# A two-layer hybrid attention block on one core: ones products in float32r pairs, a stacked gate product, scale sums on GpSimd, head openings issued one head ahead, and a reordered attention tail

## Chip, core and metric

The kernel runs on one core of one Trainium2 chip, in one launch. The metric is device microseconds (us) of an execution. TensorE is called PE here, VectorE DVE, ScalarE ACT, GpSimd POOL; SP is SyncE, which issues nearly all DMAs.

## What is computed

The reference is a block of two layers on 512 tokens of width 1024. Each layer adds a mixer of three branches to the residual stream and then a SwiGLU feed-forward. What matters here are the two linear attention branches, HGRN2 (4 heads of 128 gates and 128 values) and GLA (4 heads of 64 keys and 128 values), which share one recurrence, and the sparse branch NSA that follows them:

```
def chunked_gated_linear_attention(q, k, v, log_g):      # per head
    b = cumsum(log_g)                                    # inside a chunk
    o = (q * exp(b)) @ state + (scores with decay exp(b_t - b_s), causal) @ v
    state = exp(b_last) * state + (k * exp(b_last - b)).T @ v
y_hg  = head_rmsnorm(o_hg,  hg_norm_g)  * silu(hog)
y_gla = head_rmsnorm(o_gla, gla_norm_g) * silu(gog)
log_a = log_sigmoid(glr @ gla_w2 + gla_b) / 16           # glr: 16 columns
y_nsa = compressed + selected + window attention of 8 heads, gated
x = x + (g0*(y_hg@w_hg) + g1*(y_gla@w_gla) + g2*(y_nsa@w_nsa)) @ w_out
x = x + swiglu(rmsnorm(x))
```

## The kernel before

Activations lie transposed (features on partitions, 512 tokens along the free axis). A **dense product** is one 128x512 tile of a projection. Operands are kept as a float32r pair (a rounded part and the remainder), so each 128x128 block of weights costs three matmuls of 512 columns (`mm3`, L262 to L273). All these matmuls are chained in program order through `dense_last`. Weights come over SP as 512 KB pieces (`weights`, L167); ACT rounds a piece (`whi`, L277), DVE subtracts (`wlo`, L278), and both have two buffers.

`layer` (L519) writes the program down head by head, and a list scheduler puts each engine's instructions in order by program position and readiness; each engine then runs its list strictly in that order. Dense products are the filler: while DVE and ACT prepare a head, PE works on projections of later parts. `done` (L589, L623) is called when a head's output product is issued, and decides which projections are written there; `fill` (L568) takes steps from a list of gate and branch projections.

A head of linear attention goes so. `fit` (L361) squares the queries on ACT, sums over partitions with a product of a 128x128 matrix of ones (L368) and turns the sum into a scale. `attend` (L386) multiplies Q and K, sums the product over partitions with ones again (L399: that is the diagonal of the scores), and then works through seven levels of block sizes 1 to 64 (`gated`, L402): ACT rounds halves of K and Q to float16 (L409), DVE forms the remainders (L411) and multiplies gates into K, Q and F (L413 to L415). Levels are taken in pairs; each pair gives 24 small matmuls per head (L427), whose results DVE copies into the score tile under a mask (L433). Three links between the four chunks follow (L437 to L439), then the products of whole chunks (L445, L448) and the output product (L454). `finish` (L458) squares the output, sums it with ones (L465), and multiplies norm and gate. The buffers of a level (`ahl`) are four, so that two pairs can be ready before PE has used one.

Three of these products are plain float32: the diagonal (L399, whole 128 rows in HGRN2, two halves of 64 rows in GLA), the head norm (L465) and the scale sum (L368). The GLA decay is a float32 product over 16 rows (L616) of the low-rank projection, which `small` (L723) transposes (L751).

In NSA (`nsa`, L775) units of one head and one branch pass through scores (L919), softmax (L933), a transposing DMA of the probabilities on SP (`turn`, L952 to L955) and the products with V (`values`, L967), eight units later. After the last unit of a token block `stop` (L977) scales the block (L980) and transposes it on PE (L983). The residual x is read back over SP for the output projection (L637), as soon as its tile (shared with the NSA queries) is free.

## Time and profile before

| what | value |
|---|---|
| median of 3 runs | 1937.19 us (1936.92, 1937.19, 1939.85) |
| the profiled execution, its own time | 1939.51 us |
| its span, first to last instruction | 1937.7 us, so 1.8 us lie around it |
| mean granted TensorE clock | 0.997 |
| PE busy | 98% of the span, 10656 matmul records |
| DVE, ACT, POOL busy | 61%, 52%, 2% |
| layer 0: HGRN2, GLA, NSA | roughly 55 to 230, 230 to 345, 345 to 530 us |
| layer 1: HGRN2, GLA, NSA | roughly 1012 to 1192, 1192 to 1307, 1307 to 1490 us |

The busy time of PE is the union of records whose ends are modelled: a record of 0.39 us of a 512-column matmul overlaps the next, which starts 0.23 us later. So what a matmul costs is read from one start to the next, not from the length of its record. A matmul that was issued and could not yet run also counts as busy.

### The profile page before, as it was taken

To read this page: it belongs to the slowest core of one execution; us is meant where nothing else is said; L and a number is where in the kernel's file an instruction comes from. 1 tells how busy PE (TensorE), PEld (TensorE's weight loads), DVE (VectorE), ACT (ScalarE), POOL (GpSimd) and SP (SyncE) were. 2 spreads that over 40 slices of the span, in tenths; PEclk is the share of its full clock that TensorE was granted. 3 is DMA by queue.
4 is the path that set the end of the run, shared out by engine and by line. 5 is a ranking of instruction groups with operands and counts; after the bars stand their busy time and mean duration, and the time that the engine had idled before them with its cause. 6 is when DMAs were issued, how large, how long until landed. Compare 5 with 4: busy or idle time off the path is not lost.

```text
span 1937.7 us, 27737 instructions
## 1 busy us (share of the span) xinstructions
PE 1891.1 (98%) x10656; PEld 1361.3 (70%) x10656; DVE 1179.1 (61%) x2392; ACT 1009.0 (52%) x1815; POOL 33.5 (2%) x82
## 2 busy tenths in 40 slices
PE   8999999999999999999999999999999999999998
PEld 6778776777788544468887877767777874444787
DVE  5768767778765644423338687677896665444223
ACT  5556544377744755422245466543786457553222
POOL 0000000000000000000000000000000000000000
PEclk9999999999999999999999999999999999999999
DMA  4222211348832633113332222123487335330232
GB/s 156 77 69 86 78 57 61 109 92 158 186 94 90 209 98 107 44 60 108 109 104 66 80 77 68 64 79 96 99 169 169 98 114 190 99 106 14 76 98 96
DMA packets 142293, 194.23 MB, mean 100 GB/s; under 512 B 91408, under 2 KB 94032, under 8 KB 142160
## 3 DMA queue, kind: packets, MB, share of 16 engines
q1 hardware_dynamic: 141584, 191.80, 35.1%
q8 instruction: 84, 1.38, 0.3%
q10 hardware_dynamic: 576, 0.66, 0.1%
q14 instruction: 49, 0.40, 0.1%
HBM read 167.25 MB, written 4.19 MB: 88 GB/s over the span
## 4 chain that ended last, share of the span: by engine, by line
PE 82%; DVE 11%; ACT 3%; DMA 2%; issue 2%; SPq 0%; DVEq 0%; ACTq 0%
PE mmf L266 8%; PE mmf L264 8%; PE mmf L265 8%; PE mm L264 6%; PE mm L266 6%; PE mm L265 6%; PE mmmgate L264 4%; PE mmmgate L266 4%; PE mmmgate L265 4%; DVE wlo L278 2%; PE s L919 2%; PE o L454 2%; DVE ahl L411 2%; DMA lr<-ahl 2%; DVE at L433 1%
## 5 line engine op out<-in xcount | busy, mean ns | idle before, releaser
L277 ACT ACTIVATE whi<-wraw 128x1024 fp32r<-128x1024 f32 (+3 forms) x242 | 232.5, 961 | 359.0 <-PE mm L265 122.3
L278 DVE TENSOR_TENSOR wlo<-wraw,whi 128x1024 fp32r<-128x1024 f32 (+3 forms) x242 | 266.4, 1101 | 173.8 <-ACT whi L277 167.3
L266 PE MATMUL mmmgate<-xg,wlo 128*128 128x512 f32 x384 | 153.4, 400 | 0.4 <-DVE wlo L278 0.4
L264 PE MATMUL mmmgate<-xg,whi 128*128 128x512 f32 x384 | 153.6, 400 | 0.0
L265 PE MATMUL mmmgate<-xg,whi 128*128 128x512 f32 x384 | 153.1, 399 | 0.0
L210 DVE SCALAR_TENSOR_TENSOR whi<-xg,gsc,whi 128x1024 f16<-128x1024 f32 x38 | 48.8, 1284 | 136.0 <-ACT whi L209 136.0
L409 ACT ACTIVATE ahl<-lq 128x256 f16<-128x256 f32 x168 | 65.2, 425 | 90.3 <-DVE lq L413 57.9
L186 ACT ACTIVATE v<-xg 128x1024 bf16<-128x1024 f32 x76 | 79.9, 1051 | 32.2 <-DMA xg<-w 31.8
L264 PEld LDWEIGHTS mmmgate<-xg,whi 128*128 128x128 f32 x384 | 72.7, 189 | 17.4 <-issue 1.5
L209 ACT ACTIVATE wlo<-xg,gsc 128x1024 f16<-128x1024 f32 x38 | 43.5, 1146 | 77.6 <-PE mmf L266 77.6
L266 PEld LDWEIGHTS mmmgate<-xg,wlo 128*128 128x128 f32 x384 | 72.9, 190 | 14.9 <-DVE wlo L278 1.3
L265 PEld LDWEIGHTS mmmgate<-xg,whi 128*128 128x128 f32 x384 | 72.7, 189 | 13.6 <-issue 0.2
L948 DVE SCALAR_TENSOR_TENSOR ahl<-ld,sums,ahl 128x128 f16<-128x128 f32 (+3 forms) x128 | 66.3, 547 | 15.3 <-ACT ahl L947 14.2
L661 DVE SCALAR_TENSOR_TENSOR ld<-mmf,ginv,ld 128x512 f32<-128x512 f32 x40 | 30.0, 751 | 72.7 <-PE mmf L266 72.6
L947 ACT ACTIVATE ahl<-ld,sums 128x128 f16<-128x128 f32 (+3 forms) x128 | 65.5, 553 | 14.9 <-DMA lr<-ahl 10.6
L130 ACT ACTIVATE ld<-s,nm 128x128 f32<-128x128 f32 (+3 forms) x128 | 65.6, 517 | 13.4 <-DVE nm L938 9.4
L264 PE MATMUL mmn<-whi,xg 128*128 128x512 f32 (+1 forms) x192 | 71.3, 371 | 0.9 <-DVE og L484 0.9
L265 PE MATMUL mmn<-wlo,xg 128*128 128x512 f32 (+1 forms) x192 | 71.5, 373 | 0.0
L266 PE MATMUL mmn<-whi,xg 128*128 128x512 f32 (+1 forms) x192 | 71.5, 373 | 0.0
L411 DVE TENSOR_TENSOR ahl<-lq,ahl 128x256 f16<-128x256 f32 x168 | 67.4, 427 | 2.0 <-ACT ahl L409 1.8
L130 ACT ACTIVATE ld<-mmf,ginv 128x512 f32<-128x512 f32 x40 | 27.4, 685 | 68.9 <-PE mmf L266 68.8
L938 DVE TENSOR_REDUCE nm<-s 128x1 f32<-128x384 f32 (+3 forms) x96 | 56.3, 593 | 6.2 <-PE s L919 5.9
(433 smaller groups left out, 4964.6 us busy)
## 6 DMA issues: line engine op xcount, KB each, us to landing
wraw<-w SPq DMA_DIRECT2D x188, 512.0 KB, 3.6
xg<-w SPq DMA_DIRECT2D x76, 512.0 KB, 3.6
wraw<-w SPq DMA_DIRECT2D x57, 256.0 KB, 2.6
xt<-xT SPq DMA_DIRECT2D x16, 256.0 KB, 4.5
lr<-cw SPq DMA_DIRECT2D x16, 256.0 KB, 5.4
xd<-xt SPq DMA_DIRECT2D x8, 256.0 KB, 2.8
xt<-xd SPq DMA_DIRECT2D x8, 256.0 KB, 4.8
out<-lq SPq DMA_DIRECT2D x8, 256.0 KB, 2.6
```

The lines of the kernel that those rows point to most:

```text
L130: i = self.nc.scalar.activation(out, in_, func, **kw)
L186: self.nc.scalar.activation(self.st("v1", list(x.shape), BF), x, AF.Square, scale=scale, accum_out=ss)
L264: first = mm(out, a[0], b[0], start=start, stop=False)
L265: mm(out, a[0], b[1], start=False, stop=False)
L266: last = mm(out, a[1], b[0], start=False, stop=stop)
L277: nc.scalar.activation(hi, x, AF.Copy)
L278: nc.vector.tensor_tensor(lo, x, hi.bitcast(F32), op=ALU.subtract)
L409: nc.scalar.activation(y, x, AF.Copy)
L411: nc.vector.tensor_tensor(z, x, y, op=ALU.subtract)
L938: nc.vector.tensor_reduce(nm, pv, axis=AX.XY, op=ALU.max, negate=True)
L947: nc.scalar.activation(ahl[:, 0, b], a[:, b], AF.Copy, scale=sums[:, b:b + 1])
L948: nc.vector.scalar_tensor_tensor(ahl[:, 1, b], a[:, b], sums[:, b:b + 1], ahl[:, 0, b], op0=ALU.mult, op1=ALU.subtract)
```

## The change

- The matrix of ones becomes float32r. The HGRN2 diagonal and every head norm round their operand into a pair (one ACT copy and one DVE subtraction) and take two float32r products in place of one float32 product. The GLA diagonals stay float32.
- `fit` sums over partitions on GpSimd (`partition_all_reduce`) and needs no product.
- The small gate product becomes one float32r product over 96 rows: the transposed projection stands three times in rows 0, 32 and 64 (rounded, remainder, rounded), against weights that stand there rounded, rounded and as remainder. The weights are loaded once per layer (three DMAs of 16 KB onto a cleared tile), before it twice.
- The opening of head h+1 (scale, SiLU, gates) is written in head h's `done`, ahead of that head's own projections; the projections of Q and K move one head earlier with it.
- The gate projection of a head and the first part of its sigmoid move ahead of the levels (`outgate`), the links ahead of the last pair's products, and the output leaves PSUM earlier in `finish`.
- The NSA query transposes and the small transposes use the output's PSUM tile (`o`). In NSA a finished block is transposed after the next pair of scores, and the residual's DMAs come after the last transposing DMA.

The diff, cut to what is spoken of:

```diff
-        self.ones = self.cp.tile([P, P], F32, name="ones")
+        self.ones_r = self.cp.tile([P, P], F32R, name="ones")
+        self.ones = self.ones_r.bitcast(F32)
...
 def fit(self, xs, junk=None):
-        ps = self.pt("s", [P, n])
-        nc.tensor.matmul(ps, self.ones, acc, start=True, stop=True)
+        tot = self.st("ft", [P, n])
+        nc.gpsimd.partition_all_reduce(tot, acc, P, bass_isa.ReduceOp.add)
...
 def attend(self, Q, K, F, heads, V, gate, done):
             ps = self.pt("s", [P, T])
-            mm(ps, self.ones[p0:p1], prod[p0:p1], start=True, stop=True)
+            if p1 - p0 == P:
+                hl = [self.st("lr", [P, T], F32R) for _ in range(2)]
+                self.split(*hl, prod)
+                for n in range(2):
+                    mm(ps, self.ones_r, hl[n], start=n == 0, stop=n == 1)
+            else:
+                mm(ps, self.ones[p0:p1], prod[p0:p1], start=True, stop=True)
...
+        xs = [gate(h[2]) for h in heads]
...
             pair = [gated(L) for L in LEVELS[l0:l0 + 2]]
+            if l0 + 2 >= len(LEVELS):
+                nc.vector.tensor_copy(Q[:, 0:P], Q[:, 3 * P:])
+                nc.vector.tensor_scalar(Q[:, 3 * P:], Q[:, 3 * P:], F[:, 2 * P:2 * P + 1], None, op0=ALU.mult)
+                nc.vector.tensor_scalar(K[:, 3 * P:], K[:, 0:P], F[:, P:P + 1], None, op0=ALU.mult)
...
 def finish(self, o, g, inv, kc, xt, tag):
+        x, t = xt
-        sq = self.st("ld", [P, T])
+        sq = self.st("lr", [P, T])
         nc.scalar.activation(sq, o, AF.Square, scale=inv)
+        nc.vector.scalar_tensor_tensor(x, o, gi, x, op0=ALU.mult, op1=ALU.mult)
         ss = self.pt("s", [P, T])
-        nc.tensor.matmul(ss, self.ones, sq, start=True, stop=True)
+        hl = [self.st("lr", [P, T], F32R) for _ in range(2)]
+        self.split(*hl, sq)
+        for n in range(2):
+            nc.tensor.matmul(ss, self.ones_r, hl[n], start=n == 0, stop=n == 1)
...
+        gw2, raw = self.st("gw2", [96, 256], F32R), self.st("ld", [96, 256])
+        nc.gpsimd.memset(raw, 0.0)
+        for r in range(0, 96, 32):
+            nc.sync.dma_start(raw[r:r + 16], io["gw2"][l])
+        nc.scalar.activation(gw2, raw, AF.Copy)
+        nc.vector.tensor_tensor(gw2[64:80], raw[64:80], gw2[64:80].bitcast(F32), op=ALU.subtract)
...
+        hready, gready = [hprep(0)], []
+            def done(o, n, x):
+                if h < 3:
+                    hready.append(hprep(h + 1))
+                if h == 0:
+                    QS = self.nsa_q(Bg, rs)
+                    QK.append(pair(2))
...
-            mm(ps, gw2[:, r * P:(r + 1) * P], glrT, start=True, stop=True)
+            mm(ps, gw2[:, r * P:(r + 1) * P], small[2], start=True, stop=True)
...
         for k in range(KD):
-            nc.sync.dma_start(x[:, k], xd[:, k])
+            self.after(nc.sync.dma_start(x[:, k], xd[:, k]), self.last_turn)
...
             Y = self.st("og", [P, 8, 64])
             nc.scalar.activation(Y, Os[i], AF.Copy, scale=ni)
+            if i == NT - 1:
+                turn_y(i, Y)
...
+            else:
+                waiting.append((i, Y))
...
                 scores(*two)
+                while waiting:
+                    turn_y(*waiting.pop(), two[0]["end"])
```

**Where instructions move: PE, the norm of the last HGRN2 head and the opening of the first GLA pair, layer 0.** Before (`mmmgate` are dense products; `s_2248` is the norm sum, `s_2269` the scale sum, `s_2281` the small gate product):

```order
L266 MATMUL mmmgate_314_2207<-xg_159,wlo_2210 128x512
L465 MATMUL s_2248<-ld_2246,ones 128x512
L368 MATMUL s_2269<-fa_2264,ones 128x2
L616 MATMUL s_2281<-misc_1678,w_332_2279 128x512
L264 MATMUL mmmgate_360_2568<-xg_119,whi_2570 128x512
```

After the change, at the same norm (`s_2387`); `s_2409` and `s_2412` are the GLA diagonals, `mmgog` a gate projection:

```order
L267 MATMUL mmmgate_348_2345<-xg_159,wlo_2348 128x512
L487 MATMUL s_2387<-lr_2388,ones 128x512
L487 MATMUL s_2387<-lr_2389,ones 128x512
L406 MATMUL s_2409<-lr_2406,ones 128x512
L406 MATMUL s_2412<-lr_2406,ones 128x512
L265 MATMUL mmgog_365_2415<-xg_119,whi_2417 128x512
```

The norm is two products, the scale sum is gone from PE, the small gate product stands elsewhere, and the diagonals follow the norm at once, ahead of the gate projection that before came after the levels.

**DVE, between heads 0 and 1 of HGRN2, layer 0.** Before (`og_853`: head 0's gated output, `y_872` its remainder, `lq_263` and `lq_296`: head 1's Q and K, `ahl_905`: its first level):

```order
L475 TENSOR_TENSOR og_853<-og_853,ld_861 128x512
L461 TENSOR_SCALAR gi_1301<-fi_883,sp_68 128x1
L278 TENSOR_TENSOR y_872<-og_853,y_871 128x512
L384 SCALAR_TENSOR_TENSOR lq_263<-lq_263,fs_880,ld_885 128x512
L395 TENSOR_TENSOR ld_899<-lq_263,lq_296 128x512
L278 TENSOR_TENSOR wlo_1087<-wraw_1085,whi_1086 128x1024
L396 TENSOR_TENSOR lq_263<-lq_263,lq_891 128x512
L400 COPY_PREDICATED at_897<-imask,s_902 128x4x128
L411 TENSOR_TENSOR ahl_905<-lq_263,ahl_905 128x256
```

After (`lq_236`, `lq_238`: head 0's Q and K at its links; `lr_967`, `lr_987`: the remainders of the two float32r pairs; `lq_271`, `lq_304`: head 1's Q and K; `ahl_1030`: its first level):

```order
L431 TENSOR_SCALAR lq_236<-lq_236,lq_451 128x128
L432 TENSOR_SCALAR lq_238<-lq_238,lq_451 128x128
L482 SCALAR_TENSOR_TENSOR og_501<-o_670,gi_960,og_501 128x512
L279 TENSOR_TENSOR lr_967<-lr_962,lr_966 128x512
L396 TENSOR_TENSOR lr_982<-lq_271,lq_304 128x512
L479 TENSOR_SCALAR gi_1415<-fi_683,sp_68 128x1
L397 TENSOR_TENSOR lq_271<-lq_271,lq_691 128x512
L279 TENSOR_TENSOR wlo_718<-wraw_716,whi_717 128x1024
L279 TENSOR_TENSOR lr_987<-lr_982,lr_986 128x512
L420 TENSOR_TENSOR ahl_1030<-lq_271,ahl_1030 128x256
```

Head 1's products and first level now follow head 0's links directly; before they came after the rotation of the NSA queries and after head 0's norm was finished.

**SP, the end of NSA in layer 0.** Before (`lr<-ahl` are transposing DMAs, `xt` is the residual, `wraw` are weights):

```order
L955 DMA_TRANSPOSE lr_5468<-ahl_5465 128x8x128
L637 DMA xt_6213<-xT 128x512 x3
L171 DMA wraw_5937<-w 128x1024
L955 DMA_TRANSPOSE lr_5480<-ahl_5477 128x8x128
L955 DMA_TRANSPOSE lr_5524<-ahl_5521 128x8x128
L955 DMA_TRANSPOSE lr_5536<-ahl_5533 128x8x128
L637 DMA xt_6213<-xT 128x512
L955 DMA_TRANSPOSE lr_5580<-ahl_5577 128x8x128
L955 DMA_TRANSPOSE lr_5592<-ahl_5589 128x8x128
L637 DMA xt_6213<-xT 128x512 x3
```

After:

```order
L990 DMA_TRANSPOSE lr_5582<-ahl_5579 128x8x128
L990 DMA_TRANSPOSE lr_5594<-ahl_5591 128x8x128
L990 DMA_TRANSPOSE lr_5638<-ahl_5635 128x8x128
L990 DMA_TRANSPOSE lr_5650<-ahl_5647 128x8x128
L670 DMA xt_6271<-xT 128x512
L172 DMA wraw_5995<-w 128x1024
L670 DMA xt_6271<-xT 128x512 x7
```

All eight loads of the residual now stand behind the last transposing DMA; before, four of them stood ahead of some.

## Rows read from the trace of the kernel before

**Rows 1.** The page's line of busy time: engine, busy us, share of the span, instructions.

```profile
PE 1891.1 (98%) x10656; PEld 1361.3 (70%) x10656; DVE 1179.1 (61%) x2392; ACT 1009.0 (52%) x1815; POOL 33.5 (2%) x82
```

**Rows 2.** The page's chain that ended last, shares of the span by engine.

```profile
PE 82%; DVE 11%; ACT 3%; DMA 2%; issue 2%; SPq 0%; DVEq 0%; ACTq 0%
```

**Rows 3.** Busy time by stretch of layer 0: HGRN2, GLA, NSA to its last wait, and the stretch after that wait. Columns: stretch, its length, busy us of PE, of its weight loads, of DVE, ACT and POOL, granted TensorE clock, DMA share, GB/s.

```profile
55.00:230.00 175.00, 172.15 (x1074) 137.56 (x1073) 132.34 (x309) 98.59 (x193) 2.18 (x6) 1.00 0.24 75
230.00:345.00 115.00, 109.19 (x757) 80.40 (x756) 84.54 (x184) 59.48 (x110) 2.47 (x6) 1.00 0.22 68
400.00:523.00 123.00, 116.22 (x925) 91.83 (x924) 105.92 (x268) 99.50 (x248) 0.00 (x0) 1.00 0.74 145
523.00:530.00 7.00, 6.45 (x46) 4.76 (x46) 3.01 (x4) 3.43 (x5) 0.00 (x0) 0.51 1.07 237
```

**Rows 4.** PE's instructions in order of time around one diagonal product of HGRN2 (L399; one float32 product shows as two records). Columns: start, length, instruction.

```profile
59.99 0.40 PE L264 MATMUL mmn<-whi,xg 128*128 128x512 f32 x1
60.23 1.02 PE L399 MATMUL s<-ld,ones 128*128 128x512 f32 x2
60.69 0.80 PE L265 MATMUL mmn<-wlo,xg 128*128 128x512 f32 x1
61.32 0.39 PE L266 MATMUL mmn<-whi,xg 128*128 128x512 f32 x1
61.55 0.40 PE L264 MATMUL mmn<-whi,xg 128*128 128x512 f32 x1
```

**Rows 5.** The same view where norm, scale sum and small gate product stand together, between HGRN2 and GLA of layer 0.

```profile
229.09 0.40 PE L266 MATMUL mmmgate<-xg,wlo 128*128 128x512 f32 x1
229.32 1.02 PE L465 MATMUL s<-ld,ones 128*128 128x512 f32 x2
230.18 0.28 PE L368 MATMUL s<-fa,ones 128*128 128x2 f32 x2
230.39 1.12 PE L616 MATMUL s<-misc,w 16*128 16x512 f32 x2
231.44 0.50 PE L264 MATMUL mmmgate<-xg,whi 128*128 128x512 f32 x1
231.78 0.40 PE L265 MATMUL mmmgate<-xg,whi 128*128 128x512 f32 x1
```

**Rows 6.** Waits of PE over the whole span: who waited for whom, us in total, times, longest.

```profile
PE s L427 <- DVE ahl L411: 13.1, 20, 1.1
PE o L967 <- DMA lr<-ahl: 6.7, 6, 3.1
PE s L983 <- ACT og L980: 1.7, 2, 1.4
```

**Rows 7.** PE's instructions in order of time at the longest wait for a transposing DMA, at the end of NSA in layer 0. In brackets: idle time before, and what ended it.

```profile
520.02 0.39 PE L265 MATMUL mmmgate<-xg,whi 128*128 128x512 f32 x1
523.55 0.82 PE L967 MATMUL o<-v,lr 128*128 128x64 f16 x12 [3.14 <-DMA lr<-ahl]
...
528.12 0.63 PE L265 MATMUL mmmgate<-xg,whi 128*128 128x512 f32 x1
528.54 0.63 PE L266 MATMUL mmmgate<-xg,wlo 128*128 128x512 f32 x1
528.97 0.63 PE L264 MATMUL mmmgate<-xg,whi 128*128 128x512 f32 x1
```

**Rows 8.** SP's DMA issues in order of time before and in that wait. Columns: start of the first, time to the end of the last issue, what, how many.

```profile
504.43 9.18 SPq L955 DMA_TRANSPOSE lr<-ahl  x6
513.71 1.49 SPq L637 DMA_DIRECT2D xt<-xT  x3
515.36 0.33 SPq L171 DMA_DIRECT2D wraw<-w  x1
516.02 7.62 SPq L955 DMA_TRANSPOSE lr<-ahl  x3
523.69 0.57 SPq L637 DMA_DIRECT2D xt<-xT  x1
```

**Rows 9.** DMA issues of one line: what, queue, how many, median us from issue to landing.

```profile
lr<-ahl SPq DMA_TRANSPOSE x96, 3.4
```

**Rows 10.** Groups of instructions by line and shape over the whole span: count, busy us, mean ns of one, idle time of the engine before them and what ended it.

```profile
L278 DVE TENSOR_TENSOR wlo<-wraw,whi 128x512 fp32r<-128x512 f32 x52 | 35.7, 687 | 12.7 <-ACT whi L277 9.0 <-ACT lr L855 3.7
L277 ACT ACTIVATE whi<-wraw 128x512 fp32r<-128x512 f32 x52 | 32.7, 628 | 43.6 <-PE mmmgate L265 14.8 <-PE mmbr0d L265 12.4 <-PE mmn L266 5.9
L277 ACT ACTIVATE whi<-wraw 128x1024 fp32r<-128x1024 f32 x184 | 194.8, 1058 | 307.9 <-PE mm L265 122.3 <-issue 64.9 <-PE mmmgate L265 37.2
L411 DVE TENSOR_TENSOR ahl<-lq,ahl 128x256 f16<-128x256 f32 x168 | 67.4, 427 | 2.0 <-ACT ahl L409 1.8
L413 DVE TENSOR_TENSOR lq<-lq,lq 128x256 f32<-128x256 f32 x84 | 35.5, 423 | 0.2
L433 DVE COPY_PREDICATED at<-lm,s 128x256 f32<-128x256 uint8 x112 | 54.4, 524 | 0.4 <-PE s L427 0.4
L179 POOL PARTITION_ALL_REDUCE gtot<-gss x42 | 18.8, 447 | 794.0 <-ACT v L186 682.5 <-DVE ld L484 105.6 <-DVE y L278 5.8
```

More of the change, by code (lines that the diff above doesn't have):

```diff
@@ L99, in __init__ @@
         self.table("natural_log_exp_and_others")
-    BUFS = dict(gss=2, gtot=2, ge=2, gsc=2, ginv=3, xt=1, og=2, xg=8, wraw=2, whi=2, wlo=2, y=16, nd=3, lq=8, ld=4, g=1, nm=2, sums=6, f=2, ahl=4, lr=9, w1=2, w2=2, w3=2,
+    BUFS = dict(gss=2, fa=2, fs=2, fi=2, gtot=2, ge=2, gsc=2, ginv=3, xt=1, og=2, xg=8, wraw=2, whi=2, wlo=2, y=16, nd=3, lq=8, ld=4, g=1, nm=2, sums=6, f=2, ahl=4, lr=9, w1=2, w2=2, w3=2,
                 at=2, lv=2, v1=1, v2=1, v3=1, acc=1, rb=1, sc=1,
@@ L384, in silu_to, with attend @@
         nc.vector.scalar_tensor_tensor(out, x, s, t, op0=ALU.mult, op1=ALU.mult)
-    def attend(self, Q, K, F, heads, V, done):
+    def attend(self, Q, K, F, heads, V, gate, done):
         nc, tc = self.nc, self.tc
@@ L436, in attend @@
                         ps[:, n].rearrange("p j (g m) -> p j g m", m=L))
[L437 to L439 removed]
         outs = []
[L441 removed]
+        for (p0, p1, vc), at, x in zip(heads, ATs, xs):
             def kt(n):
@@ L581, in layer, with hprep @@
         Vh = self.evac_v(Bg("hi"), rs)
-        for h in range(4):
+        def hprep(h):
             Q, K = QK[h]
@@ L587, in layer, with gprep @@
             self.hg_gates(l, h, K, F)
[L589 to L608 removed]
+            return Q, K, F, inv
+        def gprep(r):
             Q, K = QKg[r]
@@ L621, in layer, with done @@
             self.act(F, F, AF.Exp, scale=0.0625)
-            def done(o, n):
+            return Q, K, F, inv
+        hready, gready = [hprep(0)], []
+        for h in range(4):
+            Q, K, F, inv = hready.pop(0)
+            def done(o, n, x):
+                nonlocal QS, Vg, small
+                if h < 3:
[3 more added lines that the diff above has]
+                    QK.append(pair(2))
+                if h == 1:
+                    Vg = self.evac_v(Bg("gv"), rs)
+                    QK.append(pair(3))
+                if h == 2:
+                    small = self.small(l, xg, rs)
+                    QKg.append(gpair(0))
+                if h == 3:
+                    gready.append(gprep(0))
+                    QKg.append(gpair(1))
+                if h == 3:
+                    fill(PLAN["hg"])
+                return self.finish(o, sp["hgn"][:, n:n + 1], inv, S14, x, "y")
+            yh += self.attend(Q, K, F, [(0, P, h)], Vh, lambda n: self.outgate(A("hog", n, "og")), done)
+        v12, sg, glrT = small
+        for r in range(2):
+            Q, K, F, inv = gready[r]
+            def done(o, n, x):
+                if n == 0:
+                    gready.append(gprep(1))
                 fill(PLAN["gla"][n])
-                if n == 0:
-                    QKg.append(gpair(1))
-                return self.finish(o, sp["glan"][:, n:n + 1], inv, 1.0, A("gog", n, "og"), "lq")
-            yg += self.attend(Q, K, F, [(0, 64, 2 * r), (64, P, 2 * r + 1)], Vg, done)
+                return self.finish(o, sp["glan"][:, n:n + 1], inv, 1.0, x, "lq")
+            yg += self.attend(Q, K, F, [(0, 64, 2 * r), (64, P, 2 * r + 1)], Vg, lambda n: self.outgate(A("gog", n, "og")), done)
         yn = self.nsa(l, sp, Bg, rs, QS, *v12, sg, fill, steps)
@@ L954, in turn @@
             aT = u["aT"] = self.st("lr", [P, 2, w], F16)
-            nc.sync.dma_start(aT.rearrange("p t (j c) -> p (t j) c", c=P), u["ahl"].rearrange("p t c -> p (t c)"), transpose=True)
+            ins = nc.sync.dma_start(aT.rearrange("p t (j c) -> p (t j) c", c=P), u["ahl"].rearrange("p t c -> p (t c)"), transpose=True)
+            self.last_turn = ins.ins.name
         def values(u):
@@ L980, in stop, with turn_y @@
             nc.scalar.activation(Y, Os[i], AF.Copy, scale=ni)
+            if i == NT - 1:
+                turn_y(i, Y)
+                self.hold = ins.ins.name
+                fill(1)
+            else:
+                waiting.append((i, Y))
+        waiting = []
+        def turn_y(i, Y, end=None):
             pt = self.pt("s", [P, 4, P])
             for c in range(4):
-                tp(pt[:, c], Y[:, 2 * c:2 * c + 2].rearrange("p h d -> p (h d)"), self.ident)
+                ins = tp(pt[:, c], Y[:, 2 * c:2 * c + 2].rearrange("p h d -> p (h d)"), self.ident)
+                if end is not None:
+                    self.after(ins, end)
             c = slice(i * P, (i + 1) * P)
@@ L986, in stop @@
             nc.vector.tensor_tensor(yl[:, :, c], pt, yh[:, :, c].bitcast(F32), op=ALU.subtract)
-            if i == NT - 1:
-                self.hold = ins.ins.name
-                fill(1)
         units = []
```

63 lines of the change are left out of this document (20 added, 43 removed).

## The prediction

> **What bounds the kernel now.** I read the line of busy time first: PE works 98% of the span, DVE 61% [rows 1]. The chain that ended last agrees: 82% of it is PE [rows 2]. A busy record says little about pace here, so the second view is the busy time by stretch. It shows where PE is short of full: 2.9 us in HGRN2 of layer 0, 5.8 us in GLA, 6.8 us in NSA, while DVE has 43, 30 and 17 us to spare in the same stretches [rows 3]. So PE sets the time, and a change pays in two ways: by taking work off PE, or by ending a wait of PE. Work added to DVE or ACT is paid only where PE waits for it.
>
> The third view, PE in order of time, gives prices. A dense matmul of 512 columns starts 0.23 us after the one before (61.32 to 61.55). Around a float32 ones product, 59.99 to 61.55 is 1.56 us and holds three dense matmuls, 0.69 us; the product takes 0.87 us, nearly four dense matmuls [rows 4]. The cluster at the head of GLA starts the scale sum at 230.18, the gate product at 230.39 and the next dense matmul at 231.44: 0.21 us and 1.05 us [rows 5].
>
> The fourth view is PE's waits: 13.1 us for the remainders of levels (20 times), 6.7 us for transposing DMAs, 1.7 us for the scaled NSA block [rows 6]. The longest wait is worth a look in order of time. From 520.02 the next matmul should start at 520.25 and starts at 523.55, 3.3 us late; then dense matmuls stand 0.42 us apart, not 0.23 [rows 7]. The granted clock of 523 to 530 is 0.51, the 1.2 GHz level, after PE had stood idle; in the stretches before it was 1.00 [rows 3].
>
> **The parts, priced.** Both layers are counted, 8 HGRN2 heads and 8 GLA heads in all.
>
> *Diagonal and norm.* A pair of float32r products has the shape of two dense matmuls, 0.46 us. Against 0.87 us that saves 0.41 us, for 8 diagonals 3.3 us and for 16 norms 6.6 us. They cost 24 rounds on ACT of 0.63 us and 24 subtractions on DVE of 0.69 us [rows 10], 15.1 and 16.5 us. I cost these at nothing: 8 of them per layer fall in HGRN2's heads, 5.5 us of DVE out of 43 spare, and PE has dense products in between. If that cover is gone they stand in the chain, 1.32 us each, 31.7 us in all (third rival).
>
> *Scale sums.* 14 leave PE at 0.21 us: 2.9 us. The reduction on POOL took 0.45 us on the mean in the feed-forward stage [rows 10] and stands one head ahead of its use. On POOL the clearing of a score tile is now ahead of it for later heads and waits for an output product; the head's Q comes from dense products behind that output, so nothing is added.
>
> *Small gate product.* Four float32 products of 1.05 us become one float32r matmul of 0.23 us each: 3.3 us. The tripled transposes stay four per layer. The weights' three DMAs stand on SP among weight pieces and wait for a clear on POOL; ACT's copy of them has the next weight rounds behind it. I cost both at nothing, since weight rounds wait mostly for PE to free buffers, 122.3 us for one releaser alone [rows 10]. Without that cover it is one DMA's landing per layer, some 3.4 us by the nearest row [rows 9].
>
> *The openings and links.* With head h+1's opening written ahead, DVE can build its first four levels (all buffers of `ahl`) during the dense products behind head h. The order shows it: head 1's first level directly follows head 0's links. So the first two of a head's four groups of small matmuls should find their operands ready, while levels 16 to 64 can be built only as PE frees buffers, and have fewer dense matmuls in between: in head 0 of layer 0 the order has 0, 21 and 2 between the four groups, before 12, 19 and 6. The bounds are 13.1 us gained [rows 6] and, if the shorter cover costs as much as the lookahead gives, nothing, or a loss (third rival). I take half, 6.5 us, as two groups of four are moved out of reach of the wait.
>
> *The single output tile.* The NSA query transposes now share one PSUM tile, so each of four groups waits for the one before to be read; dense products queue behind them on PE. The nearest wait of that kind took 1.4 us [rows 6]; three gaps in two layers bound it at 8.4 us, and at zero since dense products stand in between. I take zero.
>
> *The attention tail.* At 513.71 three loads of the residual (256 KB each) go out, then a weight piece, then three transposing DMAs at 516.02 to 523.64 [rows 8]; PE is released at 523.55, 7.5 us after the first of them, where a transposing DMA lands in 3.4 us on the median [rows 9]. With all residual loads behind the last transpose, that delay should go, and with it the slow stretch: 7 us at 0.51 hold 3.6 us of work, so 3.4 us are lost, of which some 0.3 us fall into the idle time already counted. 3.3 + 3.1 = 6.4 us; I take 6.0, for the weight piece stays ahead. The other waits for transposing DMAs (6.7 - 3.1 = 3.6 us) are mostly in layer 1, where the loads stand in the same way: I take 2.5 us. Bounds are nothing (the transposes' own pace) and 10 us. The loads are late by nothing that counts: ahead of the output projection stand the last gate projections and 96 dense matmuls of the third branch, over 20 us. If that failed, the first residual add would be late next.
>
> *The blocks' transposes.* Three of four per layer no longer wait for ACT: of 1.7 us I take 1.4.
>
> Sum: 3.3 + 6.6 + 2.9 + 3.3 = 16.1 us off PE; 6.5 + 6.0 + 2.5 + 1.4 = 16.4 us of waits; 32.5 us in all. From the profiled execution's 1939.51 us that leaves 1907.0 us. That execution lies 2.3 us above the median of the runs, and it holds a slow stretch that other runs may lack; I carry over half of the difference and forecast **1906 us**.
>
> **The rivals.** (1) *The waits for levels stay*, moved to the third and fourth group. For it: DVE needs for two levels four remainders, four gate products and two masked copies, at 0.43, 0.42 and 0.52 us some 4.4 us [rows 10], and the dense cover behind the second group is about that long. Against it: half the groups have an extra head's time. 26.0 us are left, 1913.5 us.
>
> (2) *The tail keeps its pace*: transposes wait for softmax and for each other, not for the residual. For it: DMA share is 0.74 in all of NSA [rows 3]. Against it: 7.5 us against 3.4. 24.0 us are left, 1915.5 us; with (1) together 17.5 us, 1922.0 us.
>
> (3) *Slower: the head's chain on DVE and ACT becomes the bound.* The float32r pairs put a round and a subtraction ahead of the diagonal and the norm, and the levels lose dense cover. If all 24 splits stand in the chain, 31.7 us come in, the 6.5 us don't, and 1939.5 - 16.1 - 9.9 + 31.7 is 1945.2 us. It decides when DVE's load in HGRN2 nears the stretch: 132 of 175 us now, 138 with the splits [rows 3]. That speaks against it; for it speaks that a wait of 3 us can also halve the clock [rows 7].
>
> (4) *The change doesn't do what it says*: PE gets no faster because dense matmuls then wait for weights, and the 16.1 us and the waits for levels come back as such. Only tail and block transposes remain, 9.9 us: 1929.6 us. Against it, weights wait for PE now [rows 10].
>
> (5) *POOL and DVE hold each other up*: 14 reductions of 0.45 us on POOL each stop a DVE instruction that a head waits for, 6.3 us at most: 1912 us. The reduction's mean of 0.45 us over 42 of them beside a working DVE shows little of it [rows 10]. The Trainium skill, SBUF — State Buffer, section "SBUF: two separate sides", says that a GpSimd instruction that reads SBUF and a DVE instruction with two SBUF inputs take one port pair by an exclusive lock, and whichever comes second is blocked for the other's whole length. By that rule the 14 reductions would cost what this rival gives; no run here shows it in the attention stage.
>
> (6) *Better: all waits named go*: 16.1 + 13.1 + 6.4 + 3.6 + 1.7 = 40.9 us, 1898.6 us. Where PE was 3.3 us late the view showed 3.14 [rows 7]; 0.16 us for each of 28 waits makes 4.5 us more, 1894 us, and with the whole difference to the median 1892.
>
> **Chances and range.** Forecast 0.50, (1) 0.14, (2) 0.12 with or without (1), (3) 0.05, (4) 0.04, (5) 0.03, (6) 0.12. The range 1892 to 1922 us reaches from (6) to (1) and (2) together; its edges and cases (3) and (4) make up the 2 in 10 outside. A measurement here can tell 0.2%, 3.9 us, from no change. All cases but (3) lie below 1933 us; I keep 0.03 for a time between. Faster 0.92, same 0.03, slower 0.05.
>
> **What the profile after would show.** Right: norm and diagonal take two records with starts 0.23 us apart, and the next dense matmul follows 0.46 us after the first; no scale sum on PE; waits for levels near 6 or 7 us; no stretch at half clock near 520 us; transposing DMAs at the end of NSA landing in 3 to 4 us. Wrong: waits for levels of 13 us or more (1), a wait over 3 us at the tail (2), PE waiting for the float32r remainders of a pair or DVE near full in HGRN2 (3), dense matmuls waiting for `wlo` (4), reductions far above 0.45 us (5).

## The result, and the profile after

The changed kernel takes 1923.48 us in the median of five runs (1921.22 to 1926.45), against 1937.74 us for the kernel before beside it (1936.92 to 1942.21): ratio 0.9922, 95% interval [0.9909, 0.9936]. The gain is 14.3 us; the forecast was 31, and its range ended at 1922. The profiled execution took 1924.03 us, with a span of 1922.2 us.

The page's busy line, which answers to [rows 1]:

```profile
PE 1876.5 (98%) x10624; PEld 1358.2 (71%) x10624; DVE 1196.0 (62%) x2420; ACT 1026.1 (53%) x1841; POOL 43.5 (2%) x100
```

The load is as forecast; nothing but PE is near full. Next PE in order of time at the first diagonal, where [rows 4] had a float32 product:

```profile
55.30 0.40 PE L267 MATMUL mmhi<-whi,xg 128*128 128x512 f32 x1
55.54 0.64 PE L404 MATMUL s<-lr,ones 128*128 128x512 f32 x2
56.02 0.40 PE L265 MATMUL mmhog<-xg,whi 128*128 128x512 f32 x1
```

From 55.54 to the next dense matmul are 0.48 us; before, the product took 0.87. So the work came off PE. The waits of PE, which answer to [rows 6]:

```profile
PE s L440 <- DVE ahl L420: 11.8, 20, 1.3
PE o L1003 <- DMA lr<-ahl: 6.2, 6, 1.9
PE s L440 <- DVE at L446: 5.5, 4, 1.4
PE o L801 <- DVE xt L806: 2.4, 4, 0.7
```

Waits for level operands are 11.8 us (13.1 before), and 5.5 us are new: small matmuls (L440) that wait for score tiles which DVE's masked copies (L446) have yet to empty. The 2.4 us at the single output tile (L801) are new too. Of the waits named in [rows 6] only the block transposes' is gone. In HGRN2 the wait moved: before, the second of a head's four groups of small matmuls waited (0.45 to 0.62 us in each of the eight heads); now the first two run together without a wait, and the third waits 0.51 to 1.31 us. The stretches that correspond to [rows 3], and one of layer 1:

```profile
55.00:230.00 175.00, 169.92 (x1075) 138.32 (x1074) 137.19 (x317) 102.08 (x198) 6.00 (x14) 1.00 0.23 75
230.00:335.00 105.00, 99.67 (x722) 74.28 (x721) 76.37 (x161) 57.56 (x100) 1.37 (x3) 1.00 0.26 79
395.00:515.00 120.00, 116.19 (x969) 91.28 (x969) 106.16 (x268) 100.73 (x249) 0.00 (x0) 1.00 0.73 149
1459.00:1466.00 7.00, 5.80 (x24) 4.74 (x25) 2.85 (x8) 2.98 (x7) 0.00 (x0) 0.52 1.07 226
```

PE is 5.1 us short of full in HGRN2 (2.9 before) and 5.3 us in GLA (5.8): lighter products, but hardly fewer waits. The half-clock stretch near 523 us is gone, and one as long stands at 1459 us in layer 1, where before there was none. PE there, in order of time (answering to [rows 7]), and SP's issues ahead of it (to [rows 8]):

```profile
1454.93 1.56 PE L1003 MATMUL o<-v,lr 128*128 128x64 f16 x48
1457.75 0.52 PE L1003 MATMUL o<-v,lr 128*128 128x64 f16 x12 [1.26 <-DMA lr<-ahl]
1460.20 0.82 PE L1003 MATMUL o<-v,lr 128*128 128x64 f16 x12 [1.93 <-DMA lr<-ahl]
...
1461.84 0.63 PE L265 MATMUL mmmgate<-xg,whi 128*128 128x512 f32 x1
1462.26 0.63 PE L266 MATMUL mmmgate<-xg,whi 128*128 128x512 f32 x1
```

```profile
1444.18 12.18 SPq L990 DMA_TRANSPOSE lr<-ahl  x7
1457.09 0.33 SPq L172 DMA_DIRECT2D wraw<-w  x1
1459.50 5.36 SPq L990 DMA_TRANSPOSE lr<-ahl  x4
1464.91 2.01 SPq L670 DMA_DIRECT2D xt<-xd  x4
```

The residual loads stand behind the last transposing DMA, as ordered. Still PE waits twice, and it waits for the last two of the seven transposing DMAs, not for the four behind them, which go out when the second wait is nearly over. The same view from 1453 us on begins with these two:

```profile
1453.74 2.62 SPq L990 DMA_TRANSPOSE lr<-ahl  x2
```

They go out 1.36 us apart, the first of them right after the softmax step that fills its source on DVE, and land 4.0 and 5.1 us after their issue, at 1457.71 and 1460.16. The median before was 3.4 us [rows 9]. Between their value products the list has no dense matmul here. In layer 0 three waits of 0.9 us are left, and two of them follow the pace of the DMAs, which land 1.42 us apart:

```profile
506.12 0.52 PE L1003 MATMUL o<-v,lr 128*128 128x64 f16 x12 [0.90 <-DMA lr<-ahl]
507.53 0.52 PE L1003 MATMUL o<-v,lr 128*128 128x64 f16 x12 [0.89 <-DMA lr<-ahl]
```

**Where the time went.** Each profiled span split in three: PE's idle time (summed over all its matmuls but the first, ahead of which 7.1 to 7.7 us pass while the first operands come), what half-clock stretches cost (length times one minus the granted clock, without the one at the end of the run), and the rest, mostly work on PE. The ratios leave out two slow executions, one of e3 and one of the kernel before.

| kernel | ratio to before, 95% | span | idle | half clock | rest |
|---|---|---|---|---|---|
| before | | 1937.7 | 32.0 | 3.4 | 1902.3 |
| changed | 0.9922 [0.9909, 0.9936] | 1922.2 | 30.9 | 3.4 | 1887.9 |
| changed, again | 0.9919 [0.9905, 0.9934] | 1923.9 | 30.4 | 5.1 | 1888.4 |
| e1 pairs alone | 0.9965 [0.9952, 0.9979] | 1930.6 | 32.8 | 5.1 | 1892.7 |
| e2 sums and gate product alone | 0.999 [0.9981, 0.9999] | 1934.9 | 34.4 | 1.7 | 1898.8 |
| e3 tail alone | 0.9955 [0.9942, 0.9968] | 1931.3 | 25.8 | 3.4 | 1902.1 |
| e4 openings alone | 0.9976 [0.9968, 0.9985] | 1933.1 | 30.2 | 1.7 | 1901.2 |
| e8 all but the openings | 0.9904 [0.989, 0.9919] | 1918.6 | 28.4 | 1.7 | 1888.5 |
| e5 changed, query on score tiles | 0.9904 [0.989, 0.9919] | 1921.4 | 28.1 | 6.8 | 1886.5 |
| e6 changed, more level buffers | 0.9909 [0.9895, 0.9923] | 1922.5 | 29.9 | 5.1 | 1887.5 |
| e12 changed, no remainders | 0.9915 [0.9901, 0.993] | 1922.1 | 26.9 | 8.5 | 1886.7 |
| e14 changed, groups later | 0.9882 [0.9866, 0.9899] | 1915.6 | 25.6 | 5.1 | 1884.9 |
| e15 changed, tail covered | 0.9913 [0.9898, 0.9928] | 1920.8 | 30.2 | 3.4 | 1887.2 |
| e16 = e5 + e14 + e15 | 0.986 [0.9846, 0.9875] | 1910.4 | 23.8 | 3.4 | 1883.2 |
| e17 = e16 and three more places | 0.9789 [0.9776, 0.9803] | 1897.8 | 13.8 | 0 | 1884.0 |
| e18 as e17, openings as before | 0.9824 [0.9811, 0.9838] | 1904.6 | 17.7 | 0 | 1886.9 |

The change took 14.4 us off the rest and 1.1 us off the idle time: the work went, the waits stayed. Two cautions belong to the table. The rest is not work alone: e14, e16 and e17 do the work of the changed kernel, and their rest is 3.0 to 4.7 us smaller. And each row is one execution, while the clock's cost varies. From the granted clocks of all executions it is, in the mean and with the stretch at the end (2.6 to 3.9 us), 5.6 to 6.5 us for the kernel before, 5.4 and 6.9 for the changed one, 6.8 in e1, 8.1 in e2 and 3.5 in e3.

### The profile page after: what moved, and what is told of

Same layout as the page of the kernel before. It is cut to its first block, busy times and chain, and to the rows that moved or that the text cites. A ratio compares the mean times of both kernels' runs of the same rounds, so it can differ in the third digit from the quotient of the medians.

```text
span 1922.2 us, 27768 instructions
## 1 busy us (share of the span) xinstructions
PE 1876.5 (98%) x10624; PEld 1358.2 (71%) x10624; DVE 1196.0 (62%) x2420; ACT 1026.1 (53%) x1841; POOL 43.5 (2%) x100
## 3 DMA queue, kind: packets, MB, share of 16 engines
q1 hardware_dynamic: 141648, 191.83, 34.4%
q8 instruction: 83, 1.36, 0.3%
## 4 chain that ended last, share of the span: by engine, by line
PE 79%; DVE 10%; issue 7%; ACT 2%; DMA 2%; POOL 0%; SPq 0%; DVEq 0%; ACTq 0%; POOLq 0%
PE mmf L267 8%; PE mmf L266 8%; PE mmf L265 8%; PE mm L265 5%; PE mm L267 5%; PE mm L266 5%; PE mmmgate L265 4%; PE mmmgate L267 4%; PE mmmgate L266 4%; PE s L954 2%; PE o L464 2%; DVE at L446 2%; DVE wlo L279 2%; DVE ahl L420 2%; DMA lr<-ahl 1%
## 5 line engine op out<-in xcount | busy, mean ns | idle before, releaser
L278 ACT ACTIVATE whi<-wraw 128x1024 fp32r<-128x1024 f32 (+2 forms) x242 | 232.6, 961 | 339.6 <-PE mm L266 116.4
L279 DVE TENSOR_TENSOR wlo<-wraw,whi 128x1024 fp32r<-128x1024 f32 (+2 forms) x242 | 266.4, 1101 | 156.3 <-ACT whi L278 148.7
L187 ACT ACTIVATE v<-xg 128x1024 bf16<-128x1024 f32 x76 | 79.8, 1050 | 23.8 <-DMA xg<-w 22.9
L130 ACT ACTIVATE ld<-s,nm 128x128 f32<-128x128 f32 (+3 forms) x128 | 65.9, 517 | 15.3 <-DVE nm L973 12.2
```

The source lines that it names most:

```text
L130: i = self.nc.scalar.activation(out, in_, func, **kw)
L187: self.nc.scalar.activation(self.st("v1", list(x.shape), BF), x, AF.Square, scale=scale, accum_out=ss)
L278: nc.scalar.activation(hi, x, AF.Copy)
L279: nc.vector.tensor_tensor(lo, x, hi.bitcast(F32), op=ALU.subtract)
```

## The experiments

**One part at a time.** e1, e2 and e3 put one part of the change into the kernel before; e4 the reordering alone.

```diff
 e1  -mm(ps, self.ones[p0:p1], prod[p0:p1], start=True, stop=True)
     +self.split(*hl, prod)                       # whole heads only; the norm likewise
     +for n in range(2): mm(ps, self.ones_r, hl[n], start=n == 0, stop=n == 1)
 e2  -nc.tensor.matmul(ps, self.ones, acc, start=True, stop=True)
     +nc.gpsimd.partition_all_reduce(tot, acc, P, bass_isa.ReduceOp.add)   # and gw2, glrT over 96 rows
 e3  -nc.sync.dma_start(x[:, k], xd[:, k])
     +self.after(nc.sync.dma_start(x[:, k], xd[:, k]), self.last_turn)     # and turn_y after the next scores
 e4   hprep/gprep, outgate and links as in the change; products, sums, query transposes and NSA as before
```

> The kernel before with one part of the change: the diagonal products of HGRN2 and the norm products as pairs of float32r products, each behind a split on ACT and DVE. Sum theory (each part brings its own term, and they add up): 9.9 us off the kernel before, ratio 0.9949, waits for level operands near the 13.1 us of before. Displacement theory (work taken off PE in HGRN2 and GLA is partly returned as waits for levels, since DVE gives the pace there): 5 to 7 us, ratio 0.9964 to 0.9974, and waits for levels of 16 us or more.

> The kernel before with two parts of the change: the attention's 14 scale sums on GpSimd, and the small gate product stacked in rows as one float32r product. Sum theory: 6.2 us off the kernel before, ratio 0.9968. Displacement theory: 3 to 4.5 us, ratio 0.9977 to 0.9985, the rest in waits for levels. If the reductions on GpSimd and DVE hold each other up, their mean is far above 0.45 us and the gain is below 2 us.

> The kernel before with one part of the change: the residual loads behind the last transposing DMA, and the transposes of NSA blocks 0 to 2 behind the next scores. Sum theory: 9.9 us (6.0 in layer 0, 2.5 in layer 1, 1.4 for the block transposes), ratio 0.9949. Pace theory (the last transposing DMAs go out 1.35 us apart and set the end by themselves where no dense matmul stands between; the residual loads only cost layer 0 its wait and half clock): 6 to 7 us, ratio 0.9964 to 0.9969, all of it in layer 0, and in layer 1 waits for transposing DMAs of 3 us as before.

> The kernel before with the reordering alone: openings one head ahead, gate projection ahead of the levels, links ahead of the last two levels (the products stay float32, the sums stay on TensorE, the gate product stays as it was, the NSA query transposes keep three score tiles, and the end of NSA stays as before). Sum theory: 6.5 us off the kernel before, ratio 0.9966, waits for levels 6 to 7 us. Displacement theory: the waits only move to the third and fourth group of a head, 11 to 15 us of them, and the time is within 3 us of the kernel before, ratio 0.9985 to 1.0015.

The pairs took 9.6 us off the rest (9.9 forecast), but gave 0.35%, 6.8 us: in the profile the half-clock cost rose by 1.7 us and the idle time by 0.8. The idle time rose at the softmax and the transposing DMAs; the waits for levels did not rise (12.7 us with the small rows), so the displacement theory had the size and not the place. Sums and gate product took 3.5 us off and gave 0.10%: waits for levels rose to 17.7 us, and over all its runs the clock cost about 2 us more than before. The tail alone gave 0.45%, 8.7 us of the 9.9 forecast. In the profile it is idle time (6.2 us), and two new stretches at half clock, of 3.4 us each, stand in GLA; four more executions of it show a higher granted clock (0.998 to 0.999, against 0.997), so part of the gain, some 2.7 us by the means above, is the clock. The openings alone gave 0.24%, of 6.5 us forecast 4.7, between the two theories: waits for operands fell to 8.5 us, and 5.4 us for masked copies were new. The four add up to 1.14%; the change gave 0.78% [0.64, 0.91]. In the profiles they add up to 20.9 us and the change has 15.5: of the 5.4 us between, 2.4 are the single tile's waits, which none of the four has, 1.7 the clock and 1.3 other idle time.

**The changed kernel again, and three edits.**

```diff
 e5  -pt = self.pt("o", [P, 4, P])          # nsa_q
     +pt = self.pt("s", [P, 4, P])
 e6  -ww = self.st("ahl", [P, 2, T], F16)
     +ww = self.st("ahl" if L < 16 else "lr", [P, 2, T], F16)
 e8   the kernel before + e1 + e2 + e3
```

> The changed kernel once more, on the chip of the next three, as their base, and for a second profile. If the stretches at half clock come from this program's own waits, the profile has one again near 1459 us in the attention of layer 1 and none near 523 us; if they come and go by chance, they stand elsewhere or are missing. Ratio to the kernel before 0.992 again.

> The changed kernel with the four transposes of the NSA queries on the three score tiles, as before, and not on the single output tile. Prediction's theory (dense matmuls hide that tile): no change against the changed kernel, within 1 us. Rival (its waits of 2.4 us are lost time): 2 us faster, and no wait of an output tile for the query's subtraction left. Second rival (the score tiles are then short for the next head's diagonal and levels): these waits come back there, and the time is the same or longer.

> The changed kernel with the pieces of levels 16, 32 and 64 in buffers of another tag (lr, 9 of them) and not in the four of ahl, so that these levels need no buffer that PE still reads. Buffer theory (prediction: levels 16 to 64 can only be built as PE frees buffers): waits for levels fall from 17.3 us to 7 us or less, and the time by 7 to 10 us against the changed kernel. DVE theory (DVE works without a pause from the norm of the last head to the third group of levels, so the levels come when DVE gets to them): waits for levels stay at 14 us or more, and the time within 3 us of the changed kernel.

> The kernel before with pairs, sums on GpSimd, stacked gate product and the end of NSA of the change, but with the openings, gate projections and links where they were, and the query transposes on the score tiles. If the parts add up as measured one by one (pairs 0.35%, sums and gate 0.10%, end of NSA 0.45%), ratio 0.991, and the reordering (0.24% by itself) is worth nothing in the changed kernel, or costs. If the reordering keeps its worth in company, ratio 0.994 to 0.995 here. Waits for levels: 18 us or more, since the kernel with the sums on GpSimd showed 17.7 us by itself.

The second profile of the changed kernel has the stretch again, at 1460.8 us, and one more of 3.4 us in GLA: the first is the program's, the other comes and goes. Three score tiles for the query took its 2.4 us of waits away (e5); the medians fell by 3.4 us, 1924.89 to 1921.51, with intervals that overlap. More buffers did nearly nothing (e6):

```profile
PE s L440 <- DVE lr L420: 10.2, 15, 1.3
PE s L440 <- DVE at L446: 5.5, 4, 1.4
```

15.7 us in place of 17.3: buffers are not what these groups wait for. And e8 is at 0.9904 without the openings, gate projections and links moved; its waits for operands are 15.3 us, where 18 or more were expected. The single gains (0.35 + 0.10 + 0.45%) add up there to within 0.1%, so in the changed kernel openings and single tile together are worth nothing, or cost 0.15%. e5, the changed kernel without the tile's waits, has the same ratio as e8: there the openings are worth nothing that can be told.

**DVE's rate, or the written order?** In the trace after, a wait in a head looks like this (PE; 22 dense matmuls lie between the groups):

```profile
197.02 1.60 PE L440 MATMUL s<-ahl 128*128 128x64 f16 x48
198.45 0.48 PE L265 MATMUL mmgq<-xg,whi 128*128 128x512 f32 x1
...
203.32 0.39 PE L265 MATMUL mmgq<-xg,whi 128*128 128x512 f32 x1
205.02 0.86 PE L440 MATMUL s<-ahl 128*128 128x64 f16 x24 [1.31 <-DVE ahl L420]
205.72 0.47 PE L266 MATMUL mmgq<-xg,whi 128*128 128x512 f32 x1
```

The first two groups run together without a wait, as forecast. The third is late, yet a dense matmul of the same projection follows it at once: it could have run first. e12 takes DVE's remainders away (it leaves out their share of the scores), e14 leaves the work and moves the groups, e15 puts dense matmuls ahead of the last value products, e16 joins e5, e14 and e15.

```diff
 e12 -nc.vector.tensor_tensor(z, x, y, op=ALU.subtract)        # remainders; products take the rounded part
 e14 -last = None
     +last = self.built if l0 >= 4 else None   # the next level's, or the links', last DVE instruction
 e15 +if k == n: fill(4)                       # ahead of values() of the last eight units, which
     +    self.after(ins, u.pop("cover"))      # in part also follow one of these dense matmuls
```

> The changed kernel without the remainders of the levels (112 to 168 subtractions of DVE per layer fall away, some 0.4 us each; the products take the rounded part three times, so PE has the same matmuls; what is left out is the remainders' share of the scores). The order of the small matmuls is redrawn when DVE has less to do: between the second and third group of the first head stand 11 dense matmuls in place of 21. DVE theory (DVE's rate in a head is what PE waits for): waits for levels fall from 17.3 us to 6 us or less, and the time by 8 us or more. Order theory (the written order puts each group just behind the point at which its operands should be ready, whatever DVE has to do, and the chip's chain is later than that by a fixed share): waits for levels stay at 10 us or more, and the time within 5 us of the changed kernel.

> The changed kernel with the same work, but the third group of levels of a head is ordered behind the building of the last level, and the last group behind the links. In the order 29 to 53 dense matmuls then stand ahead of the third group of an HGRN2 head, before 21 to 33, and the last group follows it directly. Order theory: waits for levels fall from 17.3 us to 8 us or less, the time by 5 to 10 us against the changed kernel (ratio to the kernel before 0.987 to 0.9895). DVE theory: the waits move to the far and output products behind the groups, or to the next head's start, and the time stays within 3 us of the changed kernel.

> The changed kernel with four gate projections of the third branch written ahead of the value products of the last eight units of NSA: in the order 32 (layer 0) and 23 (layer 1) dense matmuls then stand ahead of 72 to 96 value products, in place of dense matmuls behind them. Cover theory (at the end of NSA the transposing DMAs come 1.35 us apart, and PE waits because no dense matmul stands there): the waits for transposing DMAs of 6.2 us and the stretch at half clock at 1459 us go, 6 to 9 us faster than the changed kernel, ratio to the kernel before 0.987 to 0.989. Rival (the dense matmuls are then missing behind, at the block transposes and the third branch, and their weights come no earlier): the waits move there, and the time stays within 2 us.

> The changed kernel with three edits at once: the order of the third and last groups of levels, the gate projections ahead of the last value products, and the query transposes on the score tiles. If the three add up: 3 + 5 to 10 + 6 to 9 us faster than the changed kernel, ratio to the kernel before 0.981 to 0.985, 1903 to 1911 us. If the waits only change their place: 0.988 or more.

PE's waits in e12, then in e14:

```profile
PE s L438 <- ACT ahl L418: 7.8, 14, 0.8
PE s L438 <- DVE at L444: 6.0, 6, 1.4
```

```profile
PE s L442 <- DVE at L448: 5.8, 4, 1.5
PE s L457 <- DVE lq L433: 4.1, 6, 1.1
PE s L460 <- DVE at L448: 1.6, 3, 0.7
PE s L457 <- DVE lq L434: 1.3, 2, 0.7
PE s L442 <- DVE ahl L420: 0.6, 2, 0.3
```

Without the remainders DVE has less to do, and PE still waits 13.8 us, 7.8 of them now for ACT and 6.0 for DVE's masked copies: the list was redrawn, with 11 dense matmuls ahead of the third group of the first head in place of 21, and the group is again just too early. So less work on DVE alone does not end the waits; as the list changed with it, e12 does not tell rate from order by itself. e14 does, with DVE's work unchanged. With the groups later in the list the waits for operands go from 11.8 to 0.6 us and the time by 0.4%, though 5.4 us of waits appear at the far products (L457), which now follow the groups at once. The copies' wait (L442) was not touched and stayed. e15 moved only part of its wait, 6.2 to 4.8 us, and gave nothing that can be told apart: in layer 0 the last value products still waited 2.7 us, and a 7 us stretch at half clock came back at 517 us. e16 is at 0.986, 1911.55 us, against 0.981 to 0.985 expected if the three edits added up.

**The rest of the places.** In GLA the second group of levels waited for masked copies. PE, then DVE, in the changed kernel:

```profile
250.91 1.24 PE L440 MATMUL s<-ahl 64*128 64x64 f16 x60
255.12 0.88 PE L440 MATMUL s<-ahl 64*128 64x64 f16 x36 [1.39 <-DVE at L446]
```

```profile
251.01 0.69 DVE L500 TENSOR_TENSOR og<-mmgog,rb 128x512 f32<-128x512 f32 x1 [3.15 <-PE mmgog L267]
251.74 0.43 DVE L470 TENSOR_SCALAR lr<-og 128x512 f32<-128x512 f32 x1
252.08 1.22 DVE L279 TENSOR_TENSOR wlo<-wraw,whi 128x1024 fp32r<-128x1024 f32 x1
253.21 2.43 DVE L446 COPY_PREDICATED at<-lm,s 128x256 f32<-128x256 uint8 x4
```

Two heads share three score tiles, so the second group needs copies that stand behind an evacuation, the gate and a weight subtraction; only six dense matmuls lie between the groups. e17 orders that group, the far products and layer 0's last value products later; e18 does the same on e8.

```diff
 e17 -last = self.built if l0 >= 4 else None
     +last = self.built if l0 >= 4 - 2 * (len(heads) > 1) and l0 else None
     +self.after(ins, self.masked)             # ins: the first far product; masked: the last masked copy
     +if k == n + 6 and l == 0: fill(1)        # units[-1] follows its ninth matmul
```

> The kernel with the three edits at once, and three more of the same kind, no work changed: in GLA the second group of levels is ordered behind the building of the next two levels (22 and 38 dense matmuls between the first two groups, before 6), the far products behind the last masked copy, and in layer 0 the last value products behind 24 more dense matmuls. Order theory (every one of these waits is a place where the written order puts PE's step too close behind DVE's or a DMA's): of the 5.8 us of waits for masked copies, the 7.7 us at the far products and the 2.0 us for the last transposing DMA, two thirds or more go, 1900 to 1905 us, ratio to the kernel before 0.979 to 0.983. DVE theory (the head's chain is the pace): the waits come back at the output products or the next head's diagonal, 1909 to 1913 us, ratio 0.985 or more.

> The same spacing of groups, far products and value products on the kernel that keeps the openings, gate projections and links where they were before the change (pairs, sums on GpSimd, stacked gate product and the new end of NSA included). If opening one head ahead is worth something once the order leaves room, this is 3 us or more slower than the kernel with the six edits. If the order's spacing is all that counts, it is within 2 us of it, and the waits for levels are 4 us or less.

e17's waits, and the stretches of layer 0:

```profile
PE s L961 <- ACT ld L132: 3.0, 4, 1.2
PE mmn L268 <- DVE wlo L282: 2.3, 2, 1.2
PE s L445 <- DVE at L451: 2.0, 4, 0.7
PE s L465 <- DVE at L451: 1.9, 2, 1.1
PE o L1010 <- DMA lr<-ahl: 0.9, 2, 0.5
```

```profile
55.00:230.00 175.00, 172.95 (x1093) 141.75 (x1092) 140.04 (x326) 103.68 (x201) 6.07 (x14) 1.00 0.25 79
230.00:335.00 105.00, 102.85 (x741) 77.35 (x740) 76.11 (x156) 57.85 (x100) 1.89 (x4) 1.00 0.25 80
395.00:515.00 120.00, 118.24 (x986) 93.70 (x985) 102.85 (x262) 102.34 (x253) 1.15 (x1) 1.00 0.79 162
```

1899.52 us: ratio 0.9789 [0.9776, 0.9803], the fastest kernel here, and just past the end of what was expected. PE is 2.1 us short of full in HGRN2 (5.1 in the changed kernel), with more DVE work in the same stretch, not less, and no group of small matmuls waits there any more. So what PE waited for in HGRN2 was the order, and not DVE's rate. Idle time is 13.8 us, to which the 7.3 us of the start come. No stretch at half clock is left but the end of the run. e18 is at 0.9824 [0.9811, 0.9838]: the intervals are apart, and the reordering (openings, gate projections and an earlier end of `finish`, as one bundle) is worth some 0.35%, 6.8 us, once the order leaves room. How it does so is not shown. It is not by fewer waits in the heads, for ahead of NSA PE idles no longer in e18 than in e17. The 3.9 us that e18 idles more all lie in NSA, at the softmax (5.7 us against 3.0) and the transposing DMAs (2.3 against 0.9):

```profile
PE s L943 <- ACT ld L132: 5.7, 6, 1.7
PE o L992 <- DMA lr<-ahl: 2.3, 2, 1.6
```

## Why the prediction was wrong, step by step

- **What bounds.** Right: PE sets the time, and waits and work on PE are what pays.
- **Diagonal and norm, sums, gate product: 16.1 us.** Nearly right: 14.4 us left the rest. The pairs came as priced (9.6 of 9.9); sums and gate product alone gave 3.5 of 6.2. As the rest moves by up to 4.7 us without any change of work, the 1.7 us between are no finding. The splits on ACT and DVE cost nothing that shows: DVE's time in HGRN2 rose as forecast, 132 to 137 us, and e17 runs faster with them.
- **The openings and links: 6.5 us. This step failed.** The forecast took the lookahead to put two groups of four out of reach of the wait, and so half of it to be gone. That the first two groups would find their operands ready was right in HGRN2; the wait passed to the third group and grew there, from 4.3 us in eight places to 6.6. The reason given for the rest was wrong: "levels 16 to 64 can be built only as PE frees buffers" fell with e6. What e12, e14 and e17 show in its place is the list: the scheduler sets each group where it takes its operands to be ready, so operands that come earlier draw the group earlier, and a lag of some 0.6 us per place in the mean, 1.4 at most, remains. In GLA the drawing together made a new wait, for score tiles. Level groups wait 17.3 us in all, against 14.4 before (13.1 and two small rows): 2.9 us lost where 6.5 were to be won.
- **The single output tile: nothing.** Wrong by 2.4 us, within the bound of 8.4.
- **The tail 6.0, layer 1 2.5, block transposes 1.4. The tail's two terms failed too.** The block transposes went (1.7 to 0). In layer 0 the 3.14 us wait and its slow stretch went, but three waits of 0.9 us took its place; in layer 1 four waits of 3.2 us together became two long ones of 3.2 us, and brought the half clock there. Waits for transposing DMAs fell from 6.7 to 6.2 us, the half-clock cost stayed 3.4: 2.2 us of 9.9. The reading that the loads caused the wait fits layer 0, where a wait of 3 us is gone, and took for the whole cause what was one of two. The other is that these DMAs go out only when the softmax is done (SP waits 4.5 us for its last step between 1438 and 1466 us), some 1.36 us apart, and land 3.4 to 5.1 us later, at a place where the list has no dense matmul between the value products. The forecast's bound of nothing for "the transposes' own pace" named this, and its point left it out. More dense matmuls there took 1.4 us of the 6.2 us of waits in e15, and with the other edits in e17 all but 0.9; why two landings took 4.0 and 5.1 us is not shown.
- **The sum.** 32.5 forecast, 15.5 in the profile: 9.4 us missed at the levels, 7.7 at the tail, 2.4 at the tile, 1.7 at the work; some 4 us came back from smaller waits that were not counted, such as PE's for the softmax (2.8 to 1.7 us). That the time lies only 1.5 us above the range is partly these errors cancelling, and no sign that the sum was nearly right.
- **The rivals.** (1) and (2) together were given as 1922.0 us, and that is nearly what happened. (1) had the place right and gave DVE's rate as the cause, which e14 and e17 speak against. (2) was right that the transposes wait for the softmax and for each other. (3) is out: DVE is at 62%. (4) is out: dense matmuls wait 0.6 us in all for `wlo`. (5): the reductions took longer than 0.45 us, off the path; see below. (6)'s size was there to be had, by an edit that the change did not make: e17.

## What to carry to other kernels

In a program whose order a list scheduler draws, a wait of the busiest engine is often no shortage but a place where the list is too tight: look whether the instruction right behind the waiting one was ready, and if so move the waiting one back before buying buffers or taking work off the producer. Price a speed-up of a producer only after seeing where the new list puts the consumer. And measure parts in company: pairs, sums and tail added up here, the reordering's 0.24% was not to be found beside them until the order was spaced.

## What the hardware showed

**A wait can be paid twice.** At or behind waits of 1.4 to 3.1 us, or two or three shorter ones close together, stand stretches of 3.4 or 6.8 us at a granted clock of 0.50, the 1.2 GHz level, each costing 1.7 or 3.4 us: at 3.14 us in the kernel before, 1.26 and 1.93 us in the changed one, 0.77 and 0.76 us in e3 (layer 1). Many such waits have none: 1.39 us at 255 us in the changed kernel, 2.53 us at 521 us in e1, 2.65 us at 1478 us in e2. Which wait is followed by one is not worked out here. So the cost moved from place to place between kernels (0 to 8.5 us), and took back what other edits had won: in e12 4.0 us of idle time went and 5.1 us came back so.

**Reductions on GpSimd.** The change's 14 took 643 ns in the mean, against 441 ns in the feed-forward stage:

```profile
L180 POOL PARTITION_ALL_REDUCE gtot<-gss x42 | 18.5, 441 | 789.4 <-ACT v L187 678.2 <-DVE ld L500 105.4 <-DVE y L279 5.9
L369 POOL PARTITION_ALL_REDUCE ft<-fa x14 | 9.0, 643 | 150.3 <-ACT w L367 135.7 <-ACT sg L130 14.6
```

One of layer 1's, and DVE beside it:

```profile
980.49 0.93 POOL L369 PARTITION_ALL_REDUCE ft<-fa  x1 [9.89 <-ACT w L367]
```

```profile
979.95 1.22 DVE L279 TENSOR_TENSOR wlo<-wraw,whi 128x1024 fp32r<-128x1024 f32 x1
```

It ends at 981.42, 0.26 us after the subtraction of two SBUF inputs, which kept its usual length. So do ten of the 14, this one among them: they met a DVE instruction with two SBUF inputs and ended 0.24 to 0.27 us behind it. Beside an instruction that reads PSUM one took 0.38 us (100.41). The Trainium skill, SBUF — State Buffer, section "SBUF: two separate sides", has a GpSimd operation that reads SBUF and such a DVE instruction take one port pair by an exclusive lock, the later one blocked for the other's length. The trace agrees for these ten; here the later one was GpSimd, off the path. That DVE is blocked by a reduction no run shows: where such a DVE instruction followed under one (219.46 and 1169.82 us), it took its usual 0.68 to 0.69 us. So rival (5)'s mechanism is there in one direction, and its price is not.
